# A split-precision backbone kernel: order of weight splits, background steps and weight loads around the input projection

## The chip, the cores and the metric

The kernel runs on one core of a Trainium2 chip, in one launch. The metric is the device time of a run in microseconds (us); lower is better. Runs before the change: 2770.63 us median of 3 (2764.48 to 2773.29).

## What is computed

Two layers of a backbone with three gated branches (short convolution, latent attention, multi-scale pooling) run over 128 prompt tokens and 1024 sample tokens, with the same weights. Cut to what matters here:

```python
for l in range(2):                                   # for the prompt, and for the sample
    shift, scale, gate = split(silu(cond) @ w_mod[l] + b_mod[l])
    hn = rms_norm(x, g_pre) * (1 + scale) + shift
    proj = hn @ w_in[l]                              # 1024 x 7328: gates, conv, kv, q, pool inputs
    y_a = silu(a_z) * a_b * conv3(a_c * a_x)
    y_b = silu(b_z) * attention(q(rms_norm(q_down)), kv(rms_norm(kv_down)))
    y_c = silu(c_z) * (pools(c_u) @ pool_w) * pool_scale
    merged = sum(sigmoid(logits_n) * (y_n @ w_branch[n]) for n in (a, b, c))
    x = x + gate * rms_norm(merged @ w_o[l], g_post)
```

## The kernel before, in words

**Numbers in two parts.** Every matrix is held as a high and a low part. ScalarE (ACT) casts the high part (`a_copy`, line 68), VectorE (DVE) subtracts it from the value for the low part (`sub`, through `tt`, line 88). A product is three matmuls for each slice of depth (`mm3`, line 107). In the first two matmuls the high part of the weight and then its low part stand on TensorE (PE), so a product starts when the cast is done and needs the subtraction right behind it.

**The input projection** is a Strassen-like scheme in units of 256 columns, the pairs (`Pair`). `prep` is a generator that asks for the raw weights (`load`, two DMAs for each half), forms sums, and casts and subtracts them; each `next` does a step. `first` runs it up to the first half of the weight (`w[0]`), `ready` to its end. A product (`prod`, 12 matmuls of 128x512) reads one of the operands `X["11"]`, `X["21"]`, `X["22"]`, `X["T1"]` to `X["T4"]`. Ten pairs are early ones: in `early` they make the products `p1` (weight `w[0]`, operand "11") and `p2` (weight `w[1]`, operand "21"), and the prompt's. Of these `us` are the first four (layer 0) or three (layer 1), the others are `rest`. Then 19 full pairs run, and last the ten early ones again as late pairs, with five products each and no prompt. `run` does a full or late pair; behind each product `after` moves the preparation of the next pairs on (`ahead`), and for some products does a `tick`.

**Background work** is a list of generators; one `tick` moves each by a step. In `early` these are the norm of the second half of the tokens, which ends in `t_gen` (operands T1 to T4 and 22), and the prompt's norm (`hnp_gen`). In layer 0, `mid` yields between `p1` products. In layer 1, `mid` is `first` in `out_phase` and moves the norm `post_chunk` of layer 0's output. Beside the pairs run `mod_bg` (conditioning weights; a DMA of 512 KB, two yields, then four matmuls on it), `conv_gen` and behind it `s_pool` (pooling, one group after the other; each begins with `flush`, which puts all pending stores on SP's queue), `p_conv` and `p_pool` (the prompt's). `finish` runs a generator to its end at once.

**Order of work.** All instructions are issued in the order written; each engine runs its own in order. A DMA queue (SP, ACT, POOL) holds an instruction until what it stores is ready or the slot that it fills is free, and all behind it. Tiles `S` share 44 slots, the tiles in PSUM 8.

**The merges.** Before the last late pair `in_phase` finishes `conv_gen`/`s_pool` and flushes. Behind the products of that pair the hooks run: `first_w` asks for and splits the first branch weights (`w_load`, line 174, 512 KB each, and `pump`), `load_ya` copies the convolution branch's output back over POOL's queue (line 952). Then `mid_phase` runs `merge(0)` and `merge(2)`, 18 products and 18 ticks each, and beside them, from `kvq_post`, `norm` for the kv and the q latents: squares, `range(6)` yields, then the sum over partitions as a matmul with ones (`bsum`), `rstd`, scaling, splits. `kv_lat` goes on with two `rope` parts; `finish(R["first"], gp)` behind `merge(0)` runs what is left.

Of the kernel before, what the change touches and what calls it, by code (L numbers as in the profile page):

```python
# [33 lines left out]
def hybrid_step_kernel(ctx: ExitStack, tc: tile.TileContext, I, O):  # L34
# [100 lines left out]
    def spawn(gen):  # L135
        bg.append(gen)
        return gen
# [11 lines left out]
    def finish(*gens):  # L149
        for g in gens:  # L150
            for _ in g:
                pass
            if g in bg:
                bg.remove(g)
# [226 lines left out]
    def bsum(h):  # L381

        ps = PS()
        mm(ps, ones, h, True, True)
        return ps
# [298 lines left out]
    def ahead(cur, n, steps=1):  # L684

        step()
        for _ in range(steps):
            ahead1(cur, n)
# [12 lines left out]
    def ready(u):  # L701
        for _ in u.gen:
            pass
        if u in preps:
            preps.remove(u)

    def early(l, units, epis, mid, pend):

        gP, gB = pend
        nb = 4 if l == 0 else 3  # L710
        us, rest = units[:nb], units[nb:]

        def p1(u):
            u.ps1 = u.prod(u.w[0], 0, "11")

        def keep1(u, store=True):
            u.h1 = H()
            a_copy(u.h1, u.ps1)
            if store:
                act.dma_start(out=d_p1[EARLY.index(u.p)], in_=u.h1)  # L720

        def p2(u):
            v = H()
            add(v, u.prod(u.w[1], 0, "21"), u.h1)
            epis[u.p][0](0, 0, v)

        def prompt(u):
            epis[u.p][1](u.prompt())

        us[0].first()  # L730
        if l:
            for i, u in enumerate(us):
                p1(u)
                if i + 1 < nb:
                    us[i + 1].first()
                next(mid, None)
                ahead(None, 1, 2)
                keep1(u)
                step()
            ready(us[0])  # L740
        else:
            p1(us[0])
            next(mid, None)
            us[1].first()
            keep1(us[0], False)
            p1(us[1])
            next(mid, None)
            us[2].first()
            keep1(us[1], False)
            p1(us[2])  # L750
            ready(us[0])
            keep1(us[2], False)
            us[3].first()
            p1(us[3])
            next(mid, None)
            keep1(us[3], False)
        for _ in mid:
            pass
        for i, u in enumerate(us):
            ready(u)  # L760
            p2(u)
            if l == 0:
                act.dma_start(out=d_p1[EARLY.index(u.p)], in_=u.h1)
            if i + 1 < nb:
                ready(us[i + 1])
            else:
                ahead(None, 1, 3)
            if i == 1:
                rest[0].load(0), rest[0].load(1)
            tick()  # L770
        if l == 0:
            finish(gP)
            for u in us:
                prompt(u)
                ahead(None, 1, 1)
                tick()
        for i, u in enumerate(rest):
            nxt = (rest[i + 1:] or preps)[0]
            ready(u)
            p1(u)  # L780
            if l and i == 1:
                finish(gP)
            ahead(None, 1, 2)
            keep1(u)
            tick()
            nxt.load(0), nxt.load(1)
            p2(u)
            ahead(None, 1, 2)
            tick()
            late = us + rest[0:2] if l and i == 1 else [] if l and i == 0 else [u]  # L790
            for x in late:
                prompt(x)
                ahead(None, 1, 2)
                tick()
                tick()

    def run(l, u, epi, nxt=None, hooks=()):

        hooks = list(hooks)

        def after(t=False):
            full = u.kind == "full"
            ahead(u, 1 if full else 2, 1 if full else 2)
            if hooks:
                hooks.pop(0)()
            if t:
                tick()

        ready(u)
        if nxt and nxt.kind == "late":  # L810
            nxt.load_p1()
        if u.kind == "full":
            p = H()
            a_copy(p, u.prod(u.w[0], 0, "11"))
            after()
            v = H()
            add(v, u.prod(u.w[1], 0, "21"), p)
            epi[0](0, 0, v)
            after()
            epi[1](u.prompt())  # L820
            after(True)
        else:
            p = u.p1
        add(p, u.prod(u.s[1], 0, "T2"), p)
        after()
        p5 = u.prod(u.s[0], 0, "T1")
        v = H()
        add(v, p5, p)
        after(True)
        add(p, u.prod(u.s[0], 1, "T3"), p)  # L830
        w = H()
        add(w, p5, p)
        epi[0](1, 1, w)
        after()
        add(v, u.prod(u.s[1], 1, "22"), v)
        epi[0](0, 1, v)
        after(True)
        add(p, u.prod(u.w[1], 1, "T4"), p)
        epi[0](1, 0, p)
        after(True)  # L840
        for h in hooks:
            h()
# [95 lines left out]
    def in_phase(l, e, mid, pend):  # L938
        epis = pairs(l)
        u = [Pair(l, p, "full") for p in ORDER] + [Pair(l, p, "late") for p in EARLY]  # L940
        preps.extend(u)
        early(l, e, epis, mid, pend)
        if l == 0:
            spawn(gmod)
        finish(*pend)
        flush()
        ya, yp, ypc, gp = [], S(F32R), [], []

        def load_ya(m):
            ya.append((S(F32R), S(F32R)))  # L950
            for i in range(2):
                pool.dma_start(out=ya[m][i][:, 0:1024], in_=d_ya[i, m])

        def first_w():
            wlim[0] = wend[l]
            lead[0] = 3
            fill()

        g1 = g2 = None
        for i, x in enumerate(u):  # L960
            last = x is u[-1]
            hooks = []
            if last:
                finish(g1)
                flush()
                hooks = [first_w] + [lambda m=m: load_ya(m) for m in range(4)]
            if u[min(i + 1, len(u) - 1)].kind == "late":
                for y in u[i + 1:i + 3]:
                    y.load(0), y.load(1)
            if i == len(u) - 3:  # L970
                ypc.append(S(F32R))
                gp.append(spawn(p_pool(l, ypc[0])))
            run(l, x, epis[x.p], None if last else u[i + 1], hooks)
            if x.kind == "full":
                done[0] = max(x.p, done[0])
            if x.p == 8:
                done[0] = 8
            if x.p == 15:
                g1 = spawn(conv_gen(l))
            if x.p == 28:  # L980
                g2 = spawn(p_conv(l, yp))
        finish(g2)
        return ya, yp, ypc[0], gp[0]

# [243 lines left out]
    def kvq_post(l):  # L1228
# [30 lines left out]
        def norm(blocks, n, gain, outs):  # L1259
            xs = [S() for _ in blocks]  # L1260
            for x, b in zip(xs, blocks):
                sp.dma_start(out=x[:, 0:1024].rearrange("p (c x)->p c x", c=2), in_=d_kvq[b].rearrange("c p x->p c x"))
            yield
            yield
            acc = S()
            a_fn(acc[:, 0:1024], xs[0][:, 0:1024], AF.Square)
            for x in xs[1:]:
                q = S()
                a_fn(q[:, 0:1024], x[:, 0:1024], AF.Square)
                add(acc[:, 0:1024], acc[:, 0:1024], q[:, 0:1024])  # L1270
            for _ in range(6):
                yield
            pss = [bsum(acc[:, 512 * c:512 * c + 512]) for c in range(2)]
            yield
            for c in range(2):
                o = slice(512 * c, 512 * c + 512)
                r = rstd(pss[c], n)
                yield
                for k, x in enumerate(xs):
                    stt(x[:, o], x[:, o], v_(l, gain, k), r, ALU.mult, ALU.mult)  # L1280
                yield
            for k, x in enumerate(xs):
                hi, lo = outs[k]
                split(hi[:, 0:1024], lo[:, 0:1024], x[:, 0:1024])
                yield
# [559 lines left out]
    def post_chunk(l, c, O_, quick):  # L1845
# [38 lines left out]
        add(qs[0][:, 0:1024], qs[0][:, 0:1024], qs[3][:, 0:1024])  # L1884
        h2 = fold(qs[0])
        yield
        ps = bsum(h2)
        yield
        r2 = rstd(ps, DM)
# [116 lines left out]
    with tc.manual_schedule():  # L2006
# [85 lines left out]
        units[0].first()  # L2092
        finish(mod_cols(0, 2, mod0(2)))
        hn_first(0, 0, xt[0], (0, 1))
        times_r((2, 3), dve)
        gP, gB = spawn(hnp_gen(0, xp)), spawn(first_b())
        gmod = mod_bg([(0, 4), (0, 5)] + [(l, j) for l in range(1, L) for j in range(6)])
# [126 lines left out]
```

## Time and profile before

| | us |
|---|---|
| median of 3 runs | 2770.63 (2764.48 to 2773.29) |
| the profiled execution | 2769.44 |
| its span, first to last instruction | 2767.6 |
| outside the span | 1.84 |
| PE busy in the span | 2577.1 (93%) |

The span is what the views below cut into stretches. The granted clock of PE has two levels, shown as a share: 1.0 is 2.4 GHz, 0.5 is 1.2 GHz. Layer 0's early products run from 25 to 165 us and its late pairs from about 640 to 796; layer 1's early products from 1425 to 1541 and its late pairs from about 1975 to 2131.

### The profile page before, as it was taken

The page shows a single profiled execution, that of the slowest core. Times are in us where ns is not written, and L with a number is a line of the kernel's source. Part 1 is how long each engine was busy: PE and PEld are TensorE (multiplying, and loading weights), DVE is VectorE, ACT ScalarE, POOL GpSimd, SP SyncE. Part 2 cuts the span into 40 slices and gives each one's busy share as a digit, 9 for nine tenths or more (in the row PEclk, how much of TensorE's full clock was granted, in tenths as well). Part 3 has the DMA queues.
Part 4 walks back from the last instruction along what each step waited for, and adds up shares of the span by engine and source line. Part 5 has one row for each costly group of instructions (what it writes and reads, how often), then busy time and mean ns, then how long its engine had stood idle before and what let it go on. Part 6 is the DMA issues. An engine that isn't in the chain of part 4 may idle for free. (4 is left out here: it accounts for less than half of the span.)

```text
span 2767.6 us, 32478 instructions
## 1 busy us (share of the span) xinstructions
PE 2577.1 (93%) x11672; PEld 2042.7 (74%) x11672; DVE 1814.4 (66%) x2473; ACT 1108.7 (40%) x1787; POOL 762.6 (28%) x686
## 2 busy tenths in 40 slices
PE   5899999999999999899978999999998998999997
PEld 3677777776776776777867788888876777776786
DVE  4655456557757778886458544666776687888645
ACT  4532222232322357674345322323332224777531
POOL 2013311111211545653010233111111153566402
PEclk8899999999999999999999999999999999999998
DMA  7343344554587500005244322443447870000433
GB/s 269 116 134 106 101 148 159 185 198 154 195 288 282 175 5 8 24 26 181 75 148 152 103 78 72 147 160 131 166 152 262 278 256 12 5 9 31 130 110 114
DMA packets 216131, 369.96 MB, mean 134 GB/s; under 512 B 20641, under 2 KB 107681, under 8 KB 215969
## 3 DMA queue, kind: packets, MB, share of 16 engines
q1 hardware_dynamic: 175088, 280.04, 30.4%
q10 hardware_dynamic: 31968, 56.90, 5.6%
q0 software_dynamic: 8912, 30.94, 3.1%
q8 instruction: 92, 1.51, 0.2%
q14 instruction: 71, 0.57, 0.1%
HBM read 254.98 MB, written 110.66 MB: 132 GB/s over the span
## 5 line engine op out<-in xcount | busy, mean ns | idle before, releaser
L107 PE MATMUL p<-s,s 128*128 128x512 f32 (+3 forms) x10876 | 2457.7, 385 | 107.8 <-ACT s L68 56.8
L107 PEld LDWEIGHTS p<-s,s 128*128 128x128 f32 (+1 forms) x10876 | 1945.9, 190 | 595.4 <-ACT s L68 66.3
L88 DVE TENSOR_TENSOR s<-s,s 128x1024 fp32r<-128x1024 f32 (+7 forms) x582 | 625.6, 1087 | 319.1 <-ACT s L68 169.6
L68 ACT CAST s<-s 128x1024 fp32r<-128x1024 f32 (+4 forms) x368 | 359.5, 997 | 577.8 <-DVE s L88 268.3
L88 DVE TENSOR_TENSOR h<-p,h 128x512 f32<-128x512 f32 (+1 forms) x480 | 316.5, 661 | 321.2 <-PE p L107 247.1
L88 POOL TENSOR_TENSOR s<-s,s 128x512 f32<-128x512 f32 (+3 forms) x98 | 176.9, 1806 | 815.5 <-DMA s<-in_w_in_dram 629.2
L88 DVE TENSOR_TENSOR s<-h,s 128x512 fp32r<-128x512 f32 (+4 forms) x316 | 302.6, 969 | 120.0 <-ACT s L79 60.3
L79 ACT ACTIVATE h<-p 128x512 f32<-128x512 f32 (+2 forms) x364 | 208.6, 573 | 215.7 <-PE p L107 207.6
L79 ACT ACTIVATE h<-h 128x512 f32<-128x512 f32 (+1 forms) x196 | 122.8, 628 | 296.4 <-DVE h L88 252.2
L88 POOL TENSOR_TENSOR h<-h,h 128x512 f32<-128x512 f32 (+2 forms) x72 | 99.3, 1379 | 338.6 <-DVE h L88 208.0
L79 ACT ACTIVATE s<-p 128x512 fp32r<-128x512 f32 x288 | 174.2, 605 | 2.4 <-POOL h L88 2.4
L88 DVE TENSOR_TENSOR h<-h,h 128x512 f32<-128x512 f32 (+3 forms) x122 | 94.0, 771 | 106.3 <-ACT h L79 100.4
L1626 DVE TENSOR_REDUCE c<-p 128x1 f32<-128x448 f32 x256 | 147.8, 610 | 6.3 <-PE p L107 6.2
L68 ACT COPY h<-p 128x512 f32<-128x512 f32 (+1 forms) x108 | 51.6, 478 | 195.5 <-PE p L107 188.4
L88 POOL TENSOR_TENSOR s<-s 128x512 f32<-128x512 f32 x78 | 116.9, 1498 | 44.2 <-DVE s L88 43.8
L88 POOL TENSOR_TENSOR s<-h,s 128x512 fp32r<-128x512 f32 x64 | 89.2, 1394 | 126.4 <-ACT s L79 123.9
L68 ACT CAST s<-h 128x512 fp32r<-128x512 f32 (+5 forms) x92 | 47.8, 524 | 140.8 <-DVE h L88 81.1
L68 ACT COPY s<-p 64x512 f32<-64x512 f32 (+3 forms) x116 | 63.9, 567 | 56.1 <-PE p L107 55.3
L88 DVE TENSOR_TENSOR s<-p,s 128x512 f32<-128x512 f32 (+2 forms) x118 | 72.5, 630 | 15.6 <-ACT s L68 13.4
L82 POOL TENSOR_SCALAR s<-s 128x1024 fp32r<-128x1024 f32 (+1 forms) x40 | 51.2, 1286 | 89.6 <-ACT s L68 51.8
L88 POOL TENSOR_TENSOR s<-s,h 128x512 f32<-128x512 f32 x20 | 30.7, 1533 | 132.1 <-DVE h L100 92.0
L103 POOL TENSOR_SCALAR s<-s,cols 128x512 f32<-128x512 f32 x16 | 14.8, 934 | 167.8 <-ACT s L79 167.8
(121 smaller groups left out, 972.3 us busy)
## 6 DMA issues: line engine op xcount, KB each, us to landing
s<-in_w_in_dram SPq DMA_DIRECT2D x304, 256.0 KB
s<-in_w_mod_dram SPq DMA_DIRECT2D x48, 512.0 KB
d_gate<-h ACTq DMA_DIRECT2D x96, 256.0 KB
s<-d_gate SPq DMA_DIRECT2D x64, 256.0 KB
s<-in_w_br_dram SPq DMA_DIRECT2D x24, 512.0 KB
d_part<-s SPq DMA_DIRECT2D x48, 256.0 KB
s<-in_xT_dram SPq DMA_DIRECT2D x16, 512.0 KB
s<-d_ya POOLq DMA_DIRECT2D x16, 512.0 KB, 8.0
```

Source lines behind the costliest of these rows:

```text
L68: act.copy(out=out, in_=in_)
L79: act.activation(out=out, in_=in_, func=func, scale=scale, bias=bias)
L82: pool.tensor_scalar(out=out, in0=in_, scalar1=1.0, scalar2=0.0, op0=ALU.mult, op1=ALU.add)
L88: eng.tensor_tensor(out=out, in0=in0, in1=in1, op=op)
L103: (eng or dve).tensor_scalar(out=out, in0=in0, scalar1=s1, scalar2=s2, op0=op0, op1=op1)
L107: pe.matmul(out=out, lhsT=lhsT, rhs=rhs, start=start, stop=stop)
L1626: dve.reduce_max(out=mv[:, i, qt:qt + 1], in_=ps[:, 0:448], axis=AX.X)
```

## The change

- `early`, layer 1: between the `p1` products the second weight halves of `us[0]` and `us[1]` are split with `ready`, in place of `ahead` steps.
- `early`, layer 0: pair 1's first half is split during the setup, those of pairs 2 and 3 behind the first product, the second halves of pairs 0 and 1 between the `p1` products.
- `early`, both: in the loop of `p2`, the next pair is made ready before `p2(u)`, and with that before the sum that follows it, instead of after.
- `run`: a late pair does a `tick` behind each of its five products, instead of behind three.
- `in_phase`: `p_conv` starts eight places before the end of the list of pairs, that is behind the third late pair, instead of behind the last full one; the first two weights of the merge are asked for before the last pair.
- `norm` waits 9 yields instead of 6 before its `bsum`; `post_chunk` yields once more before its own where it isn't the quick one.

```diff
@@ early, layer 1
                 if i + 1 < nb:
                     us[i + 1].first()
+                if i != 1:
+                    ready(us[i // 2])
                 next(mid, None)
-                ahead(None, 1, 2)
                 keep1(u)
                 step()
-            ready(us[0])
@@ early, layer 0
             p1(us[0])
             next(mid, None)
-            us[1].first()
+            us[2].first()
+            us[3].first()
             keep1(us[0], False)
             p1(us[1])
+            ready(us[0])
             next(mid, None)
-            us[2].first()
             keep1(us[1], False)
             p1(us[2])
-            ready(us[0])
+            p1(us[3])
+            ready(us[1])
             keep1(us[2], False)
-            us[3].first()
-            p1(us[3])
+            keep1(us[3], False)
             next(mid, None)
-            keep1(us[3], False)
@@ early, loop of p2
         for i, u in enumerate(us):
-            ready(u)
-            p2(u)
-            if l == 0:
-                act.dma_start(out=d_p1[EARLY.index(u.p)], in_=u.h1)
             if i + 1 < nb:
                 ready(us[i + 1])
             else:
                 ahead(None, 1, 3)
+            p2(u)
+            if l == 0:
+                act.dma_start(out=d_p1[EARLY.index(u.p)], in_=u.h1)
@@ run, after
-            if t:
+            if t or not full:
                 tick()
@@ in_phase
-            if x.p == 28:
+            if i == len(u) - 8:
                 g2 = spawn(p_conv(l, yp))
+            if i == len(u) - 2:
+                wlim[0] = wend[l]
+                w_load()
+                w_load()
@@ norm
-            for _ in range(6):
+            for _ in range(9):
                 yield
@@ post_chunk, before bsum(h2)
         h2 = fold(qs[0])
         yield
+        if not quick:
+            yield
         ps = bsum(h2)
@@ setup
         hn_first(0, 0, xt[0], (0, 1))
+        units[1].first()
         times_r((2, 3), dve)
```

## Rows read from the trace of the kernel before

**Rows 1.** The page: span, busy time of each engine (share of the span).

```profile
span 2767.6 us, 32478 instructions
PE 2577.1 (93%) x11672; PEld 2042.7 (74%) x11672; DVE 1814.4 (66%) x2473; ACT 1108.7 (40%) x1787; POOL 762.6 (28%) x686
```

**Rows 2.** Busy time by stretch: length, engines (instructions), PE clock, DMA share, GB/s.

```profile
25.00:95.00 70.00, 41.23 (x143) 26.57 (x143) 30.22 (x48) 29.45 (x39) 13.94 (x14) 0.70 0.45 162
1424.00:1477.00 53.00, 32.08 (x102) 22.70 (x101) 33.75 (x44) 20.36 (x30) 4.89 (x11) 0.77 0.40 140
2000.00:2131.00 131.00, 122.32 (x504) 97.07 (x502) 93.07 (x138) 40.51 (x60) 23.12 (x30) 0.95 0.55 182
2062.50:2099.00 36.50, 36.50 (x159) 29.60 (x160) 26.58 (x33) 11.41 (x16) 6.32 (x8) 1.00 0.55 185
```

**Rows 3.** Waits, 25 to 95 us: who for whom, us, times, longest.

```profile
PE p L107 <- ACT s L68: 24.1, 6, 8.4
```

**Rows 4.** Waits, 1430 to 1480 us.

```profile
PE p L107 <- ACT s L68: 17.6, 4, 8.4
```

**Rows 5.** Timeline of PE, 20 to 100 us: start, us, instruction, [idle before, releaser].

```profile
38.23 2.81 PE L107 MATMUL p<-s,s 128*128 128x512 f32 x11 [0.76 <-DVE s L88]
...
71.90 5.06 PE L107 MATMUL p<-s,s 128*128 128x512 f32 x11 [0.47 <-DVE s L88]
...
94.24 0.79 PE L107 MATMUL p<-s,s 128*128 128x512 f32 x1 [7.54 <-ACT s L68]
```

**Rows 6.** Timeline of all engines, 0 to 96 us: ACT's part.

```profile
58.71 3.90 ACT L79 ACTIVATE s<-s 128x1024 f32<-128x1024 f32 x4
...
87.53 1.29 ACT L79 ACTIVATE h<-h 128x512 f32<-128x512 f32 x2
...
93.15 1.04 ACT L68 CAST s<-s 128x1024 fp32r<-128x1024 f32 x1 [0.88 <-ACT h L79]
```

**Rows 7.** Timeline of all engines, 1380 to 1482 us: ACT's part.

```profile
1440.27 0.63 ACT L79 ACTIVATE h<-h 128x512 f32<-128x512 f32 x1
...
1441.30 1.04 ACT L68 CAST s<-s 128x1024 fp32r<-128x1024 f32 x1 [0.40 <-ACT h L79]
```

**Rows 8.** Timeline: PE at four sums over partitions (ones), DVE at a rope.

```profile
1391.44 2.05 PE L107 MATMUL p<-h,ones 128*128 128x512 f32 x2 [3.00 <-DVE h L88]
...
831.30 1.88 PE L107 MATMUL p<-s,ones 128*128 128x512 f32 x4
...
861.76 3.23 PE L107 MATMUL p<-s,ones 128*128 128x512 f32 x4 [2.79 <-DVE s L88]
...
2197.10 3.60 PE L107 MATMUL p<-s,ones 128*128 128x512 f32 x4 [4.36 <-DVE s L88]
...
869.39 3.81 DVE L88 TENSOR_TENSOR h<-h,h 32x512 f32<-32x512 f32 x4 [0.51 <-DMA h<-in_cosT_dram]
```

**Rows 9.** Timeline at the merges' start: PE twice, SP's weights, POOL's copies.

```profile
802.10 0.79 PE L107 MATMUL p<-s,s 128*128 128x512 f32 x1 [6.27 <-ACT s L68]
...
2135.25 0.57 PE L107 MATMUL p<-s,s 128*128 128x512 f32 x1 [4.50 <-ACT s L68]
...
2125.09 7.23 SPq L174 DMA_DIRECT2D s<-in_w_br_dram  x5
...
2115.34 1.18 POOL L952 DMA_DIRECT2D s<-d_ya  x2 [6.65 <-PE p L107]
```

**Rows 10.** Late pairs: PE's timeline, DVE's, and a wait of SP's queue (640 to 810).

```profile
684.96 1.92 PE L107 MATMUL p<-s,c 128*32 128x512 f32 x4 [6.00 <-DMA s<-in_w_mod_dram]
...
2026.99 28.00 PE L107 MATMUL p<-s,s 128*128 128x512 f32 x108 [3.52 <-DVE h L100]
...
2112.00 1.22 PE L107 MATMUL p<-s,h 128*128 128x512 f32 x2 [4.19 <-ACT s L68]
...
2085.18 2.49 DVE L88 TENSOR_TENSOR s<-s,s 128x512 f32<-128x512 f32 x2 [8.22 <-POOL s L88]
...
SPq L130 <- DVE h L88: 36.2, 6, 11.7
```

## The prediction

> **What bounds the kernel now.** I read the page first. PE is busy 2577.1 of 2767.6 us; its weight loads, which overlap it, take 74%, no other engine more than 66% [rows 1]. So the time is PE's, and only what PE waits for, or does at its lower clock, can be won: at most 190 us of idle time, and this over all stages. Next I listed PE's idle stretches and the granted clock by stage. In the full pairs there is hardly a gap; the gaps sit in the early products of both layers, in the late pairs, at the start of the merges and at the sums over partitions. The change touches all of these and little else, so I read those stretches one by one: first the busy times [rows 2], then the waits [rows 3, 4], then the timeline [rows 5 to 10].
>
> The reader is to see two things. In the early products of layer 0 PE waits 24.1 us for casts by ACT, in those of layer 1 17.6 us [rows 3, 4], while neither ACT nor DVE is full there: DVE works 30.22 of 70 us and 33.75 of 53 [rows 2]. They are late by order, not by load: the cast at 1441.30, which the next product needs, stands on ACT behind the sigmoid of 1440.27, and that waits for a sum of the product in front [rows 7]. And behind a wait PE works at 1.2 GHz for a while: 11 matmuls that take 2.81 us at the full clock take 5.06 [rows 5].
>
> **The change part by part.** All terms are made against the profiled execution, 2769.44 us, which is the span and 1.84 us around it; the median of the runs is 1.2 us above it.
>
> *Early products, layer 0.* To win: 24.1 us of waits, and four products at the lower clock, 2.25 us each (5.06 less 2.81 [rows 5]): 33 us. No instruction is added; casts (1.04 us, [rows 6]) and subtractions move forward. What is late next: the background norm of the second half of the tokens. Its four squares take ACT 3.90 us at 58.71 [rows 6], and its sum over partitions stands on PE ahead of the second `p2`. Today PE's own lateness covers them; then it doesn't. I estimate that PE stands 8 us at that sum: the squares, and about as much for the additions behind them. Further, the split for the fourth `p2` stays behind the logarithm and exponential of that norm. These end at 88.82, its cast starts at 93.15 [rows 6]; so of PE's wait of 7.54 us [rows 5] 4.3 go and 3.2 stay. With 4.5 us of lower clock behind the two, and 4 us for the second halves of the weights, whose splits now stand ahead of the operand "21", 33 - 8 - 3.2 - 4.5 - 4 = 13 us are won. Bounds: 6 us, if only the two longest waits are shortened by a third (16 us in all); 22, if the sum's wait is mostly hidden.
>
> *Early products, layer 1.* To win: 17.6 us and three products at the lower clock, 6.7 us: 24. The first and longest wait, 8.4 us [rows 4], goes, since that cast now stands ahead of the background step. The later casts still stand behind a step each of the norm; PE comes to them earlier and waits for what is left. DVE has 33.75 us of work in these 53 [rows 2], so at most 19 can go. I take half, 9; bounds 4 and 15.
>
> The mean granted clock of the two stretches is 0.70 and 0.77 [rows 2]; by the products I count 16 us for that (9.0 and 6.7). The Trainium skill, "TensorE: Matmul & The Clock Gate" (Part 1: The HAM clock gate, and Terms), has the clock low by default and released by activity, and prices a stretch at the low clock at half of it; that would be 33 us here, and up to 17 us more to win. The rows decide: part of the low-clock time is idle anyway.
>
> *The sums over partitions.* PE stands 2.79, 4.36 and 3.00 us at three of them, 10.2 in all, and works longer behind: 3.23 and 3.60 us where 1.88 do at the full clock, and 2.05 where half of 1.88 should do [rows 8], 4.2 more. One yield more (`post_chunk`) or three (`norm`) put one or three products ahead of the sum; that covers these waits. The price: `kv_lat` has 18 yields ahead of its ropes instead of 15, and `merge(0)` gives 18 steps, so both ropes instead of one fall into `finish`, each 3.81 us of DVE [rows 8] ahead of the sums of `merge(2)`. Twice, that is 0 (PSUM lets PE go on) to 7.6 us. I take 3.4: 11 us won, bounds 4 and 15.
>
> *The merges' weights.* PE waits 6.27 and 4.50 us for the cast of the first branch weight; its load was given out at 2125.09, 10 us before [rows 9], because SP's queue stood behind the stores of `s_pool` (line 130, 36.2 us in the late pairs of layer 0 [rows 10]). Asked for before the last pair, two loads go out a pair earlier. With some 2.5 us of lower clock at each, 16 us can be won. What is late next are the eight copies of `load_ya`: POOL gives them out as PE frees slots (6.65 us of wait ahead of two of them [rows 9]), and nothing in the change brings them forward. I take half, 8; bounds 0 and 16.
>
> *A tick with each late product, and `p_conv` later.* The waits of 3.52 us (a PSUM bank that `p_conv` holds while DVE waits) and 4.19 us (matmuls of `s_pool` dumped by `finish`) should go, since `s_pool` is now through before the last pair; also 6.00 us at a load of `mod_bg` may change [rows 10]. With lower clock 21 us could be won. Against this: background steps come 5/3 as often. Where PE had no wait, DVE was busy 26.58 of 36.5 us [rows 2], 73%. If a quarter of that is background, it becomes some 85%, and more where `p_conv` falls on `s_pool`. DVE already stands 8.22 us for POOL where raw weights come late behind SP's stores [rows 10]. And `mod_bg` has two ticks from load to use: a late pair's 60 matmuls take 13.8 us (36.50 for 159 [rows 2]), so two ticks were 9.2 us and become 5.5, while the row at 684.96 shows a load that landed 6 us after PE came to it. Four such loads fall into late pairs of layer 0. I take 0 for the whole: it is nearest to the rows on both sides. Bounds: 21 won, 22 lost (each of four late-weight stretches passes 5.5 us on to PE).
>
> *At nothing:* pair 1's early split in the setup (ACT and DVE wait for loads there; 2.3 us if they don't), and the `ahead` steps left out in layer 1 (`ready` does them).
>
> Sum: 13 + 9 + 11 + 8 + 0 = 41 us; 2769.4 - 41 = **2728 us**. All bounds at their good ends give 89 us, at their bad ends a gain of 14 and a loss of 22, 2777 us; neither is likely.
>
> **Rivals.**
>
> *The waits move on.* The chains of norms on ACT and DVE set the pace of the early products, PE only arrives sooner at the same casts. For it: the sums that stood hidden [rows 6]. Against: DVE's free time there [rows 2]. A third of the early terms (7), half of the sums (6), a third of the merges' (3): 16 us, 2753 us.
>
> *The copies decide the merges.* POOL's copies of `load_ya` wait for PE, not for SP [rows 9], so they end when they did; if PE's first product waits for them, the merges give nothing, 2736 us. Against: the DMA engines are busy only 0.55 of the last pairs [rows 2]. The rule beside it: the Trainium skill, "DMA: Bandwidth & Descriptors" (Issuing engines are not separate DMA queues), says that loads of all issuers interleave on the same 16 DMA engines, so weights asked for earlier would only share with what is on its way.
>
> *No change.* What the early products win is waited off later, at the first full pair, whose weights' loads wait for slots: 2769 us, within 8 us (0.3%, about what a measurement of this kernel can tell from no change). Against: those slots are freed by PE's own products, so they come earlier too.
>
> *Slower.* DVE becomes the bound of the late pairs. Place: the pairs in which two groups of `s_pool` and `p_conv` run. Price: PE then waits for the splits of the next pair; at 20% over, the 20 late pairs of 13.8 us cost 55 us, against 41 won: 2783 us. It decides from the point where a late pair has over 15.7 us of DVE work (41 us over 20 pairs on top of 13.8), against 10 now (73%). That would take more background work than there is in all of them, so it is unlikely.
>
> **Chances.** Forecast 0.52 (2728), copies 0.12 (2736), waits move on 0.20 (2753), no change 0.09, slower 0.07. The first three are faster by over 0.3%: 0.84; the same 0.09; slower 0.07. The range leaves out the last two cases and the far ends of the others: from 2702 (26 more than the sum: the early terms and the late pairs near their good ends) to 2757 (waits moved on, with 4 more lost).
>
> **What would show it.** Early products: PE's waits for ACT casts of 24.1 and 17.6 us fall to some 12 and 8, a new wait of about 8 us for DVE stands ahead of the first sum over partitions in layer 0, and the products behind run at the full clock sooner. Sums: no wait ahead of the three; if ropes matter, a longer wait than now early in `merge(2)`. Merges: the weights' loads go out a pair before; what PE then waits for is named DMA of `d_ya`. Late pairs: DVE's share rises over 80% while `s_pool` runs and falls behind it; the waits at 2026.99 and 2112.00 are gone; waits on the loads of `mod_bg` come up to four times. Wrong it would be made by DVE idle times behind POOL that pass to PE in the late pairs, or by early products that end no sooner than now.

## The result and the profile after

The changed kernel takes 2722.66 us (median of 4 runs, 2720.12 to 2729.05) against 2769.89 before (2764.48 to 2773.29): a ratio of 0.9835 with a 95% interval of 0.9811 to 0.9858, 47 us less. The forecast was 2728 us, 41 less. The profiled execution took 2720.12 us.

The page after, span and busy times (share of the span):

```profile
span 2718.2 us, 32466 instructions
PE 2555.8 (94%) x11672; PEld 2032.0 (75%) x11672; DVE 1821.4 (67%) x2473; ACT 1108.9 (41%) x1787; POOL 764.8 (28%) x686
```

Against [rows 1] the span is 49.4 us shorter: PE's busy time is 21.3 less with as many matmuls (fewer of them at the lower clock: the granted clock of the profiled execution is 0.974, that of the kernel before 0.967), its idle time 28.1.

To see where, I counted PE's matmuls in the trace of each kernel. All have 11672, in much the same order, so the time from matmul number a to number b is that of the same stretch of work. In us; the last four columns are experiments 2 to 5, told below, in which parts of the change are undone:

```
stretch (matmul numbers)               before  after  early0  early1  ticks  weights+ticks
                                                       _old    _old    _old   _old
early products, layer 0    0 -  260     95.4    75.9    95.7    76.9    74.6   76.1
(untouched)              260 - 2900    546.0   546.5   546.0   546.6   546.4  546.6
late pairs, merge start 2900 - 3540    165.4   156.6   160.8   160.9   162.1  164.5
merge(0), merge(2)      3540 - 3900     94.9    93.6    95.7    93.8    98.2   95.7
attention               4560 - 5020    116.9   119.4   114.1   119.4   111.8  112.7
sum in post_chunk       5700 - 6000     75.6    71.1    71.2    71.1    71.1   71.1
early products, layer 1 6000 - 6180     63.8    57.9    56.4    65.1    56.4   56.4
first full pair         6180 - 6560     70.9    73.7    71.4    73.8    74.3   74.1
late pairs, merge start 8700 - 9240    147.0   138.5   139.1   137.3   137.5  147.4
merge(0), merge(2)      9240 - 9700    120.4   116.6   115.4   116.7   122.7  117.2
attention              10100 -10700    148.7   143.7   146.4   143.7   146.3  145.4
```

So layer 0's early products gave 19.5 us, those of layer 1 5.9 (with 2.8 lost at the first full pair), the late pairs with the merges' starts 8.8 and 8.5, the sums 1.3, 4.5 and 3.8. The table also tells how far a small difference may be believed: the attention, which no edit touches, differs by up to 7.6 us between kernels. And each column is one execution, the profiled one: that of experiment 2 was the fastest of its five runs, that of experiment 3 the slowest of its four.

Early products of layer 0 after: PE's waits, 25 to 80 us, and PE's timeline. They answer to [rows 3, 5].

```profile
PE p L107 <- DVE h L88: 9.0, 1, 9.0
PE p L107 <- ACT s L68: 5.5, 1, 5.5
PE p L107 <- DVE s L88: 2.9, 5, 1.6
PE p L107 <- ACT s L79: 1.6, 1, 1.6
```

```profile
40.13 7.90 PE L107 MATMUL p<-s,s 128*128 128x512 f32 x32
...
59.18 2.04 PE L107 MATMUL p<-h,ones 128*128 128x512 f32 x2 [9.04 <-DVE h L88]
...
74.66 0.80 PE L107 MATMUL p<-s,s 128*128 128x512 f32 x1 [5.52 <-ACT s L68]
```

The casts are there in time now, and 32 matmuls run without a gap. The new wait of 9.04 us is the one forecast (8) ahead of the sum over the second half of the tokens; the last wait for a cast went from 7.54 to 5.52 (3.2 forecast).

Early products of layer 1 after: PE's waits, 1390 to 1445 us, PE's timeline, and the busy times from 1390 to 1445. They answer to [rows 2, 4, 8].

```profile
PE p L525 <- POOL s L103: 6.9, 1, 6.9
PE p L107 <- ACT s L68: 6.3, 2, 5.1
```

```profile
1364.50 1.10 PE L107 MATMUL p<-h,ones 128*128 128x512 f32 x2 [0.32 <-DVE h L88]
...
1393.72 11.64 PE L107 MATMUL p<-s,s 128*128 128x512 f32 x48
1412.28 1.97 PE L525 MATMUL p<-ident,s 128*128 128x128 f32 x8 [6.92 <-POOL s L103]
...
1425.15 0.80 PE L107 MATMUL p<-s,s 128*128 128x512 f32 x1 [5.09 <-ACT s L68]
```

```profile
1390.00:1445.00 55.00, 39.24 (x137) 28.92 (x136) 37.07 (x48) 26.31 (x38) 5.64 (x13) 0.81 0.43 148
```

The sum of `post_chunk` that waited 3.00 us [rows 8] comes one product later and waits 0.32 (1364.50). The waits for casts fell from 17.6 to 6.3 us, but a wait for POOL, for the prompt's scaling ahead of its transposes, has taken the place of the first.

Late pairs and merges after: PE's timeline, from stretches of 600 to 2110 us. They answer to [rows 8 to 10].

```profile
715.50 2.05 PE L107 MATMUL p<-s,h 128*128 128x512 f32 x3 [5.99 <-ACT s L68]
...
782.11 8.81 PE L107 MATMUL p<-s,s 128*128 128x512 f32 x37 [0.42 <-DMA s<-d_ya]
...
840.64 1.88 PE L107 MATMUL p<-s,ones 128*128 128x512 f32 x4
...
855.06 13.46 PE L107 MATMUL p<-s,s 128*128 128x512 f32 x48 [6.98 <-DVE s L88]
...
2035.64 2.05 PE L107 MATMUL p<-s,h 128*128 128x512 f32 x3 [7.23 <-ACT s L68]
```

The wait for the first branch weight (6.27 us) is gone; 0.42 us for `d_ya` is left. In layer 1 the 4.50 us are gone and 0.62 are left. In its place in the late pairs stand 5.99 and 7.23 us at matmuls of `s_pool`, and at 855.06, the start of `merge(2)`, a wait of 6.98 us. DVE has 32.60 us of work in the 38 from 2012 to 2050, 86%; from matmul 8700 to 8900 its share was 71% before and is 86% now. The busy times of that stretch:

```profile
2012.00:2050.00 38.00, 30.73 (x122) 24.02 (x121) 32.60 (x50) 12.53 (x20) 10.63 (x6) 0.87 0.45 156
```

### The profile page after: what moved, and what is told of

Read it like the earlier page. It is cut to its first block, busy times and chain, and to the rows that moved or that the text cites. A ratio compares the mean times of both kernels' runs of the same rounds, so it can differ in the third digit from the quotient of the medians.

```text
span 2718.2 us, 32466 instructions
## 1 busy us (share of the span) xinstructions
PE 2555.8 (94%) x11672; PEld 2032.0 (75%) x11672; DVE 1821.4 (67%) x2473; ACT 1108.9 (41%) x1787; POOL 764.8 (28%) x686
## 3 DMA queue, kind: packets, MB, share of 16 engines
q1 hardware_dynamic: 175088, 280.04, 31.5%
## 4 chain that ended last, share of the span: by engine, by line
PE 69%; DVE 12%; issue 4%; ACT 4%; DMA 4%; POOL 1%; SPq 0%; ACTq 0%; DVEq 0%; POOLq 0%
PE p L107 69%; DVE s L88 7%; DVE h L88 2%; DVE c L1629 1%; ACT s L68 1%; ACT h L79 1%; ACT s L79 1%; DMA s<-d_ya 1%; DMA s<-d_kvq 1%; DMA s<-in_w_in_dram 0%; DVE s L100 0%; DVE h L100 0%; DMA s<-d_gate 0%; DVE c L1636 0%; DVE h L103 0%
## 5 line engine op out<-in xcount | busy, mean ns | idle before, releaser
L88 DVE TENSOR_TENSOR s<-s,s 128x1024 fp32r<-128x1024 f32 (+5 forms) x582 | 621.7, 1082 | 243.3 <-ACT s L68 136.2
L88 POOL TENSOR_TENSOR h<-h,h 128x512 f32<-128x512 f32 (+2 forms) x72 | 97.9, 1360 | 343.6 <-DVE h L88 218.3
L88 DVE TENSOR_TENSOR h<-h,h 128x512 f32<-128x512 f32 (+3 forms) x122 | 99.5, 816 | 105.6 <-ACT h L79 96.9
L107 PE MATMUL p<-s,h 128*128 128x512 f32 (+1 forms) x184 | 55.6, 415 | 15.9 <-ACT s L68 15.8
```

What stands on the lines that cost most here:

```text
L88: eng.tensor_tensor(out=out, in0=in0, in1=in1, op=op)
L107: pe.matmul(out=out, lhsT=lhsT, rhs=rhs, start=start, stop=stop)
```

## The experiments

All edits are made to the changed kernel, and each was timed beside the kernel before. Ratios are to that kernel; the changed kernel stands at 0.9835. "Theory" and "rival" are those of the expectation ahead of each result.

**1. The early requests for the merge's weights taken out.**

```diff
-            if i == len(u) - 2:
-                wlim[0] = wend[l]
-                w_load()
-                w_load()
```

> The changed kernel (2722.7 us) without the two early requests for the merge's weights. Theory, from the traces of before and after: the request a pair ahead is worth its whole price at both merges, so the waits of 6.27 and 4.50 us for the first cast come back, with some 2.5 us of lower clock behind each: 16 us more, 2739 us. Rival, the forecast's half: the copies hold part of the gain anyway, 8 us more, 2731 us. Second rival, the copies alone decide: no change, within 4 us of 2723.

2724.78 us, ratio 0.9839 (0.9826 to 0.9853): next to nothing, and within 0.3 us in both stretches of late pairs and merge start. The theory fell, and so did the forecast's half; the waits did not come back. The second rival's number came, but not for its reason: PE waits 0.46 us for the copies.

```profile
783.03 8.82 PE L107 MATMUL p<-s,s 128*128 128x512 f32 x37 [0.46 <-DMA s<-d_ya]
```

**2. Layer 0's early products in the old order.** (The old lines of the block, the loop of `p2` and the setup, for layer 0 alone.)

> The changed kernel with layer 0's early products in the old order: the split of pair 1 not in the setup, the splits between the p1 products and in the loop of p2 as before. Theory: the gain of 18.5 us which the traces show at equal places stays in the kernel to the end, so it is lost here: 2741 us, with a wait of 7 to 8 us for a cast ahead of the fourth p2 again and no wait for DVE ahead of the sum of the second half of the tokens. The forecast had 13 for it: 2736 us. Rival: the waits move on, and the first full pair or the late pairs take back most of it: 2729 us or less.

2744.86 us, ratio 0.9911 (0.9898 to 0.9925): 22 us lost, the theory; the profiled execution, 2736.58 us, lost 16 in all and 19.8 in the stretch. PE's waits in the stretch, and its busy times (the changed kernel's follow):

```profile
PE p L107 <- ACT s L68: 25.1, 6, 8.4
PE p L107 <- DVE s L88: 4.8, 7, 0.8
PE p L107 <- ACT s L79: 1.6, 1, 1.6
...
25.00:98.00 73.00, 42.83 (x146) 27.76 (x147) 32.06 (x50) 29.60 (x40) 13.89 (x14) 0.72 0.43 156
```

```profile
25.00:80.00 55.00, 36.43 (x150) 24.16 (x151) 32.42 (x51) 30.11 (x41) 11.82 (x14) 0.78 0.57 203
```

DVE and ACT do the same work in both; PE is busy 6.4 us longer for four matmuls fewer, at a granted clock of 0.72 against 0.78.

**3. Layer 1's early products in the old order.**

```diff
-                if i != 1:
-                    ready(us[i // 2])
                 next(mid, None)
+                ahead(None, 1, 2)
                 keep1(u)
                 step()
+            ready(us[0])
```

(and the old loop of `p2`, for layer 1 alone)

> The changed kernel with layer 1's early products in the old order. Theory: the chain of the norm on ACT and DVE sets the pace there, PE only stands at other instructions, so 3 us more at the end of the first full pair, 2726 us. Rival, the forecast: the splits ahead are worth 9 us, 2732 us, and the waits for ACT's casts go from 6.3 back to 17.6 us with no other wait in place of them.

2724.57 us, ratio 0.9843 (0.9828 to 0.9859): 1.9 us by the medians, less than they can tell from none. In the profiled execution the stretch itself is 7.2 us longer (65.1 against 57.9), nearer to the forecast's 9 than to the theory's 3; the first full pair takes 73.8 either way, so what is lost there does not come from this part. But that execution took 2731.61 us, the other three 2722.51 to 2724.70: whether the stretch was as long in them, and why the time hardly shows it, stays open.

**4. A tick behind three of five late products, `p_conv` behind the last full pair.**

```diff
-            if t or not full:
+            if t:
...
-            if i == len(u) - 8:
+            if x.p == 28:
                 g2 = spawn(p_conv(l, yp))
```

> The changed kernel with a tick behind three of the five products of a late pair, and p_conv started behind the last full pair, as before. Theory: the denser ticks won the waits of 3.52 and 4.19 us of layer 1 and lost as much at the matmuls of s_pool, which now come four ticks of 2.8 us behind their split (waits of 5.99 and 7.23 us): within 5 us of 2723, and in the trace those two pairs of waits change places. Rival: the denser ticks make DVE so full that late weights cost PE time; then this kernel is 10 us or more faster, 2713 us. Second rival: they win, and the old order costs 8 us or more, 2731 us.

2725.76 us, ratio 0.9845 (0.9831 to 0.9858): by the time, the theory. By stretches more moves: 10.1 us lost in layer 0 from matmul 2900 through the merges and 5.1 in layer 1 from 8700 through the merges, covered in part by an attention 7.6 us shorter in layer 0. How much of this is the ticks' and how much `p_conv`'s later start, no run separates. The waits for `finish`'s dump and for the load of `mod_bg` (5.84 us) are back, and at the merge PE waits for the copies:

```profile
780.08 0.74 PE L107 MATMUL p<-s,s 128*128 128x512 f32 x2 [2.09 <-DMA s<-d_ya]
782.67 4.62 PE L107 MATMUL p<-s,s 128*128 128x512 f32 x13 [1.85 <-DMA s<-d_ya]
...
2076.50 1.22 PE L107 MATMUL p<-s,h 128*128 128x512 f32 x2 [4.19 <-ACT s L68]
```

**5. Both undone: edits 1 and 4 together.**

> The changed kernel without the early requests for the merge's weights and with a tick behind three of five late products and p_conv later, as before: both parts undone at once. Undone singly they moved the time to 2724.8 and 2725.8 us, so little. Theory: either of the two is enough to bring the merge's weights in time, because what held their loads back was the stores of s_pool that stand ahead of them on SP's queue: the ticks get these out of the way, and the early request is put ahead of them. Undone together, the waits of 6.27 and 4.50 us for the first cast come back with their lower clock: 2741 us. Rival: the two parts have nothing to do with each other, the waits at the merges went for another reason (the shifts of the stages ahead): 2728 us, no wait over 2 us at the merges' start.

2736.19 us, ratio 0.9884 (0.9866 to 0.9901): 13.5 us lost where the two singly lose 2.1 and 3.1; the six runs lie from 2726.80 to 2743.52. The theory, by its waits and nearer by its time. In the stretches of late pairs and merge start it is 7.9 and 8.9 us. PE waits for the first casts again, as in [rows 9]:

```profile
782.78 0.79 PE L107 MATMUL p<-s,s 128*128 128x512 f32 x1 [6.19 <-ACT s L68]
...
2104.99 0.66 PE L107 MATMUL p<-s,s 128*128 128x512 f32 x1 [4.43 <-ACT s L68]
```

SP's queue shows why. First the changed kernel, then edit 1, edit 4 and both (the stores of `s_pool` are line 130, the weights line 174; a group's time runs from its first to its last request):

```profile
747.11 23.38 SPq L174 DMA_DIRECT2D s<-in_w_br_dram  x5
```

```profile
748.00 23.38 SPq L174 DMA_DIRECT2D s<-in_w_br_dram  x5
```

```profile
753.37 1.15 SPq L174 DMA_DIRECT2D s<-in_w_br_dram  x2
769.92 2.37 SPq L130 DMA_DIRECT2D d_yc<-h  x2
772.38 4.65 SPq L174 DMA_DIRECT2D s<-in_w_br_dram  x3
```

```profile
769.70 2.36 SPq L130 DMA_DIRECT2D d_yc<-h  x2
772.16 7.32 SPq L174 DMA_DIRECT2D s<-in_w_br_dram  x5
```

With the dense ticks `s_pool` puts its last stores on the queue at 730 us, SP runs ahead of PE, and the requests go out from 747 or 748 on, whichever line asks for them. Without the ticks the early lines put two requests ahead of the stores, at 753. Without either all five stand behind the stores until 772, as before the change (there until 791.62 us). So either part ends the wait for the first cast. That the two don't add in time is shown by the medians alone: by places, from 2900 and 8700 through the merges, edit 1 loses 1.5 us, edit 4 15.2 and both 19.5, so that undoing the ticks alone costs most of it there, through the waits shown in edit 4.

**6. The yields ahead of the sums as before.**

```diff
-            for _ in range(9):
+            for _ in range(6):
...
-        if not quick:
-            yield
         ps = bsum(h2)
```

> The changed kernel with 6 yields in norm and without the second yield in post_chunk. Theory, from the traces at equal places: the three waits come back (2.79, 4.36, 3.00 us and the lower clock behind: 16 us) and the waits behind merge(0), 6.98 and 6.25 us, fall to about 3 each (9 us won): 7 us more, 2730 us. Rival, the forecast as it stood: 11 more, 2734 us. Second rival, the ropes cost nothing and the waits behind merge(0) stay: 16 more, 2739 us.

2726.24 us, ratio 0.9851 (0.9838 to 0.9864): 3.6 us lost, less than each theory said. `post_chunk`'s sum waits 3.02 us again, and its stretch (5700 to 6000) takes 76.6 us against 71.1. But from 3540 to 3900 the kernel takes 93.9 against 93.6, from 9240 to 9700 116.3 against 116.6: the three yields of `norm` give nothing. Of the 2.79 us at `q_lat`'s sum only 0.32 came back, and of the 6.98 us at the start of `merge(2)` 5.21 stayed:

```profile
832.35 1.98 PE L107 MATMUL p<-s,ones 128*128 128x512 f32 x4 [0.32 <-DVE s L88]
...
853.79 12.95 PE L107 MATMUL p<-s,s 128*128 128x512 f32 x48 [5.21 <-DVE s L88]
```

**7. The ropes spread over the ticks of `merge(2)`.**

```diff
-        finish(R["first"], gp)
+        finish(gp)
...
-        finish(*R["second"])
+        finish(R["first"], *R["second"])
```

> The changed kernel, with kv_lat not finished behind merge(0): it goes on with the ticks of merge(2) and is finished behind that. Theory: the waits of 6.98 and 6.25 us at the start of merge(2) are DVE's eight rope instructions (7.83 us for seven of them) in a row ahead of the sums that free PSUM; a tick apart they hide: 12 us less, 2711 us. Rival: the ropes push the sums of merge(2) back wherever they stand, as DVE is near full there: less than 4 us won, 2719 us or more.

2716.59 us, ratio 0.9816 (0.9803 to 0.9829). In the place itself the rival: the start of `merge(2)` (3720 to 3780) takes 14.3 us in place of 21.8, and the next products (to 3900) 38.0 in place of 29.3, with waits for DVE of 0.98, 1.03 and 5.34 us; in layer 1 9.3 for 18.3 and 55.0 for 46.3. (These are matmuls 9460 to 9500 and 9500 to 9700.) Nothing is won there. That the shorter time is the edit's doing is not shown: the profiled execution, the slowest of the four, has a span of 2718.6 us, the changed kernel's 2718.2, and the intervals of the two ratios overlap.

**8. The ropes' multiplications on POOL.**

```diff
-                mul(kr[c][r0:r0 + 32, :], x[r0:r0 + 32, :], t[r0:r0 + 32, :])
+                mul(kr[c][r0:r0 + 32, :], x[r0:r0 + 32, :], t[r0:r0 + 32, :], eng=pool)
```

(and the same for the one into `t`)

> The changed kernel with the eight multiplications of the ropes on POOL instead of DVE (they still run in a row behind merge(0)). Spread over the ticks of merge(2) they gave little: DVE had 32.6 to 34 us of work in each 40 there, and the wait came back 20 us later. Theory: it is DVE's work that PE waits for at the start of merge(2), not the place of the ropes; POOL stands idle for 46 us there, so 8 us of work off DVE in each layer take away most of the waits of 6.98 and 6.25 us: 10 us less, 2713 us. Rival: the wait comes back at another instruction of DVE, as it did then: less than 4 us won, 2719 us or more.

2718.41 us, ratio 0.9818 (0.9803 to 0.9832); in the place the rival: 18.2 and 35.8 us in layer 0 (2.9 more than the changed kernel), 10.1 and 53.3 in layer 1 (1.2 less). DVE, now without the ropes, waits 7.29 us for the load of the first gate, and a few products later it is slow. DVE's timeline, layer 0:

```profile
854.37 0.69 DVE L88 TENSOR_TENSOR s<-p,s 128x512 f32<-128x512 f32 x1 [7.29 <-DMA s<-d_gate]
...
871.69 0.68 DVE L88 TENSOR_TENSOR s<-p,s 128x512 f32<-128x512 f32 x1
872.29 5.97 DVE L100 SCALAR_TENSOR_TENSOR s<-s,vec,h 128x512 f32<-128x512 f32 x3
```

The multiplication at 854.37 frees PE's first PSUM bank, and it comes no sooner than in the changed kernel, where the ropes' row ends at 854.28:

```profile
846.45 7.83 DVE L88 TENSOR_TENSOR h<-h,h 32x512 f32<-32x512 f32 x7 [0.28 <-DMA h<-in_sinT_dram]
```

The loads of these gates go out from 847.90 on, behind `merge(0)`'s last stores and the ropes' own loads on SP, into DMA engines that are busy 0.99 of the time from 850 to 860.

**9. Seven yields in `s_pool` between the split and the matmuls on it.**

```diff
-            for _ in range(4):
+            for _ in range(7):
                 yield
             pg = slice(128 * gi, 128 * gi + 128)
```

> The changed kernel with 7 yields instead of 4 in s_pool between the split and the matmuls that read it. Theory: the waits of 5.99 us in layer 0 and 2.57 and 7.23 us in layer 1 at those matmuls come only from the denser ticks (four of them are 11 us in a late pair); three ticks more, 8 us, cover them and the lower clock behind: 18 us less, 2705 us. Rival: DVE is the bound in these late pairs (32.6 of 38 us busy), so PE stands at the next split instead: less than 5 us won, 2718 us or more.

2712.23 us, ratio 0.9798 (0.9785 to 0.9811): the shortest time measured, 10.4 us less, between the two. The waits at `s_pool`'s matmuls are gone, as the theory has it (64.8 us for 72.4 from 2960 to 3240, 87.9 for 97.9 from 8700 to 9060). But `s_pool`'s last matmuls come 25 us later in layer 0 and 17 in layer 1, and at the merges more is lost than was won, 13.3 us from 3240 to 3540 and 11.0 from 9160 to 9240:

```profile
778.46 1.81 PE L107 MATMUL p<-s,s 128*128 128x512 f32 x3 [4.90 <-DMA s<-d_ya]
...
2089.90 1.19 PE L107 MATMUL p<-s,s 128*128 128x512 f32 x2 [5.25 <-DMA s<-d_ya]
```

In the profiled execution the attention (4560 to 5020), 8.7 us shorter, more than makes up for it. The time is thus not shown to come from the edit.

**10. The same by degrees:** `range((4, 4, 6, 7)[gi])`.

> The changed kernel with 4, 4, 6 and 7 yields in s_pool's four groups in place of 4 in each. With 7 in each the waits at s_pool's matmuls went (11 us won in layer 0, some 16 in layer 1), but s_pool ended 28 us later, and behind the last pair PE waited 4.90 and 5.25 us for the copies of d_ya. Theory: these copies get their slots late because s_pool holds slots and POOL longer; with five ticks more instead of twelve both gains stay: 2707 us, no wait over 2 us for d_ya. Rival: the copies' time hangs on PE's own pace, so whatever the late pairs win is waited off at d_ya: the same 2712 us.

2720.28 us, ratio 0.9828 (0.9814 to 0.9842): both theories missed. The wait at `d_ya` is 0.87 us, but PE waits 3.98 us for a load of `mod_bg`, 2.71 us at `s_pool` and 4.02 us for a load of `p_pool`, that of 3.92 us in layer 1 too. Each of the three paces tried puts PE behind another load.

**11. Two edits in the early products.** In layer 0 `first_b` yields three times instead of once ahead of its sum, in layer 1 `hnp_gen` gets 3 gaps instead of 2.

```diff
             h = norm_x(1)
             yield
+            yield
+            yield
             ps = bsum(h)
...
-            yield from hnp_gen(l + 1, out, 2)
+            yield from hnp_gen(l + 1, out, 3)
```

> The changed kernel with two edits in two stages, read apart at equal places in the trace. Layer 0: two yields more ahead of the sum over the second half of the tokens. Layer 1: one yield more ahead of the prompt's transposes. Theory: in layer 0 the wait of 9.04 us ahead of the sum is only a matter of order, as the p2 products behind it are ready, and the cast waited for 5.52 us stands behind that norm's logarithm: 10 us less. In layer 1 the wait of 6.92 us for POOL covers another one, for the casts behind ACT's and DVE's norm chain (its cast at 1413.08 came when POOL was done): under 2 us. In all 2711 us. Rival for layer 0: DVE and ACT are full, PE waits for the casts instead: under 3 us. Rival for layer 1: the transposes' wait was the forecast's missing gain: 6 us less.

2714.91 us, ratio 0.9802 (0.9789 to 0.9816), 7.8 us less. Layer 0's part is in its place: 68.7 us to matmul 260 in place of 75.9, with 1.0 given back to 640; the wait of 9.04 is gone, and 1.44 and 2.90 us for casts are left. In layer 1 nothing is won (58.6 for 57.9): PE's wait for POOL turns into one for a cast, as the theory has it.

```profile
1389.14 11.70 PE L107 MATMUL p<-s,s 128*128 128x512 f32 x48
1409.58 0.80 PE L107 MATMUL p<-s,s 128*128 128x512 f32 x1 [8.74 <-ACT s L68]
```

**12. Edit 9, edit 8 and layer 0's edit of 11 together.**

> The changed kernel with three of the edits that won by themselves: 7 yields in all of s_pool's groups (2712.2 us by itself), the ropes' multiplications on POOL (2718.4) and two yields more ahead of the sum over the second half of the tokens in layer 0 (part of 2714.9). Theory: they act in different stages and add: 10.5, 4.3 and some 6 us, 2702 us. Rival: what one stage wins the next waits off, as at the copies of d_ya behind the late pairs and at the loads of the conditioning weights: half of it, 2711 us.

2717.00 us, ratio 0.982 (0.9806 to 0.9834): the gains don't add; by its median it is slower than edit 9 alone, though the intervals touch. The early products keep theirs (68.9 us to matmul 260), the late pairs and merges are as in 9 and 8, and the attention takes 5.2 and 7.1 us more than in 9 (115.9 and 150.8).

## Why the prediction was right, and where not

The sum was right: 41 us forecast, 47 measured. Undone, the parts lose 22.2 (early products, layer 0), 1.9 (layer 1), 3.6 (sums) and 13.5 us (weights and ticks together) by the medians, 41.2 of the 47.2; in their own stretches 19.8, 7.2, 5.5 and 16.8. That the sum came so close was partly luck: against the forecast's 13, 9, 11 and 8, two terms are 9 and 5.5 us too small by the medians and two 7 and 7.4 too large, and this cancels.

**Early products, layer 0: right, mis-sized.** 13 us were forecast, 20 to 22 are measured. The new wait of about 8 us came as 9.04. Wrong was what I held back for the lower clock and the second halves of the weights. PE's waits fell from 31.5 us (25.1 + 4.8 + 1.6, edit 2) to 19.0 (9.0 + 5.5 + 2.9 + 1.6), 12.5 us, and its busy time by 6.4: 18.9. The second halves cost nothing visible; 4 us were charged for them. The clock gave 6.4 where 4.5 net was counted (9.0 less 4.5). The split in the setup, put at nothing, was worth some 2.4 of the 18.9: the waits of 1.65 and 0.76 us (the second at 38.23 in [rows 5]) at pair 1's first product are gone. The 1.65 stood in the 24.1 to be won all the same. PE at that product, before and after:

```profile
36.97 0.50 PE L107 MATMUL p<-s,s 128*128 128x512 f32 x1 [1.65 <-ACT s L68]
```

```profile
35.54 3.05 PE L107 MATMUL p<-s,s 128*128 128x512 f32 x12
```

**Early products, layer 1: 9 forecast, 5.9 and 7.2 in the stretch, 1.9 by the medians.** Too much by either; the time alone does not show this gain (experiment 3). That DVE's free time bounds the gain was the weak step: it is not full even now, 37.07 of the 55 us from 1390 to 1445, and still the chain of norms on ACT and DVE sets the pace. Edit 11 shows it: PE's wait for POOL, once moved, is one of 8.74 us for a cast. The prediction's reading of [rows 7] missed this. The sigmoid of 1440.27 did not wait for a sum, which was there at 1436.78. In front of it ACT stood 4.37 us for DVE at a square of the norm, went on with the norms, and loaded a table of functions (1.28 us). The kernel before, ACT's timeline:

```profile
1435.26 1.06 ACT L79 ACTIVATE s<-s 128x1024 f32<-128x1024 f32 x1 [4.37 <-DVE s L88]
...
1438.98 1.28 ACT L79 ACT_TABLE_LOAD   x1 [0.39 <-ACT h L68]
```

**Sums: 11 forecast, 3.6 to 5.5 measured, all of it `post_chunk`'s.** The waits went at all three, as said, but in `norm` they were not worth their rows: PE, let go there, came sooner to the start of `merge(2)`. The price was put on the ropes (3.4), and a longer wait did come there, the forecast's sign for them. That cause was only partly right: edits 7 and 8 take the ropes from the place, and it gives nothing back. Where the ropes' multiplications are taken off DVE (edit 8), the load of the first gates holds the place, which goes out on SP behind the stores of `merge(0)`.

**Merges' weights 8 and ticks 0: together 13.5 to 16.8, and by the medians not parts of a sum.** The wrong step was to give the merges' gain to the early request. SP's queue runs ahead of PE, so what counts is what stands ahead of a request, not where PE is when it is written down. The stores of `s_pool` stood ahead; the denser ticks take these away, and the early request passes them. Either brings the first weight in time (edits 1, 4, 5). The half taken off for the copies was wrong for this kernel: PE waits 0.42 us for them. They are next in line, though: 4.90 and 5.25 us once `s_pool` runs longer (edit 9). The Trainium skill, "DMA: Bandwidth & Descriptors" (Issuing engines are not separate DMA queues), says that the DMAs of all issuers interleave on the same 16 engines. From this the prediction drew that weights asked for earlier would only share them; the traces don't bear that conclusion out, as the wait for the weights went. The rule itself is not tested here.

**Late pairs.** The waits of 3.52, 4.19 and 6.00 us went and DVE's share rose over 80%, as forecast. Putting the whole at 0 was too low by places: with the old ticks 15.2 us are lost from the late pairs through the merges, though 3.1 by the medians (edit 4). What was paid for the denser ticks was a distance counted in ticks: four yields between the split and the matmuls of `s_pool` became about 11 us (four products of some 2.8), and 5.99, 2.57 and 7.23 us of waiting stood there. With seven yields they go (edit 9). Waits on the loads of `mod_bg`, feared at four places with up to 5.5 us, show at one, and there differ from kernel to kernel (2.36 us, put down to DVE, in the changed one, 3.98 in edit 10). The *Slower* rival's limit of 15.7 us should read 15.85 (41 us over 20 pairs is 2.05, on top of 13.8); nothing hangs on it.

Open: why the attention differs by up to 10 us between kernels that don't touch it (110.7 to 120.5 us from matmul 4560 to 5020 over all runs). The traces show what goes with it: the granted clock there is 0.985 in edit 9 (110.7 us), 0.97 where it takes 111.8 to 114.3, 0.956 at 115.4 to 116.9, and 0.943 where it takes 119.4 or more, and PE stands idle 6.6 us in the shortest and 13.0 in the longest. Whether this belongs to a kernel or to an execution isn't shown, as each kernel has one trace; executions of one kernel differ by as much (2726.80 to 2743.52 us in experiment 5). With it stays open what the 10.4 us of edit 9 are.

## What to carry to other kernels

A delay written in background steps is a delay in time only as long as the steps keep their pace: who makes ticks denser must look at every generator that counts on so many of them, and who shortens a stage at the loads that were just early enough for it. Before a load is asked for earlier, see what stands ahead of it in its issuer's queue; getting a store out of the way can bring the load in time as well as the earlier request does, and the same wait can't be won twice. And to tell where some microseconds went, compare the times between equal instructions of two traces: the medians alone would have credited edits 7 to 9 with gains that their own places don't show. One trace is one execution, though, and a stretch that no edit touches tells how far to trust it.

## What the runs showed of the hardware

Instructions of DVE that read two tiles take longer while POOL works on tiles. In edit 8 three of DVE's products of two tiles take 5.97 us beside POOL's additions (872.09 to 877.7), in the changed kernel, with POOL idle, 2.07:

```profile
876.86 2.07 DVE L100 SCALAR_TENSOR_TENSOR s<-s,vec,h 128x512 f32<-128x512 f32 x3
```

An instruction that reads one tile and PSUM keeps its 0.68 us in both. Work moved to an idle POOL is so partly paid for by DVE. From matmul 9240 to 9700 the eight rope multiplications taken off it had 8.3 us, but its other 110 instructions there, the same in both kernels, take 86.4 us instead of 80.1. The Trainium skill, "SBUF — State Buffer" (SBUF: two separate sides), says that a DVE instruction with two SBUF inputs and a GpSimd instruction that reads SBUF lock each other out of a shared pair of ports for a whole instruction. The rows agree that DVE is held up, at 1.99 us against 0.69 for one; why it is DVE that waits each time, and not POOL, whose additions keep their 1.3 us, they don't show.
